# A float32r decoder trunk on one core: 448 unused bytes placed in front of the activation tiles

## The chip, the cores and the metric

The kernel runs on one core of a Trainium2 chip, in one launch. The metric is the device time of one execution in microseconds (us), as the median of several runs. One further execution was recorded by the hardware profiler; all engine times below come from that one. TensorE multiplies matrices, VectorE and ScalarE do elementwise work, GpSimd sets up a small table, and SyncE's queue issues the transfers from the chip's main memory. All of them read their operands from the on-chip memory, which has 128 partitions; a tile takes the same bytes in each partition, so its place is given as a byte within a partition.

## The reference

What is computed is a trunk of four residual layers on 256 tokens of 1024 channels, in float32. Each layer has a token mixer and then a gated convolutional channel mixer (FFN), each with a norm before and after:

```
h = x
for i in range(4):
    a = rms_norm(h, mix_norm_pre[i])
    m = (dilated_attention, short_conv, conformer_conv)[i % 3](a)
    h = h + rms_norm(m, mix_norm_post[i])
    u = causal_dwconv(rms_norm(h, ffn_norm_pre[i]) @ w_in, w_conv)   # width 3
    g, v = split(u)                                                 # 2816 channels each
    h = h + rms_norm((silu(g) * v) @ w_out, ffn_norm_post[i])
```

Layers 0 and 3 mix tokens by attention in three groups of 16 heads (windows 128, 512 and 2048, dilations 1, 4 and 16), whose outputs are weighted by their log-sum-exp. Layer 1 uses a gated convolution of width 3, layer 2 a gated convolution of width 31 with a layer norm. Nearly all of the arithmetic is in the products with the weight matrices.

## The kernel before, in words

Channels lie on the 128 partitions and the 256 tokens along them. A product of the layer's input with a weight matrix is therefore a sum over 8 tiles of 128 input channels (22 in the second FFN product): for each, TensorE loads 128 x 128 weights, and then streams the 128 x 256 inputs past them into a bank of the accumulator memory. The operand that is loaded is called the weights (`lhsT`), the other the stream (`rhs`). For accuracy each float32 operand is split into two float32r parts, `hi` and `lo`, and each product is made of three: hi x hi, hi x lo and lo x hi.

**Weights.** `Stream` (line 145) brings them in, in the order of their use: SyncE's queue loads blocks of 1 MB into one of three `raw` tiles; ScalarE copies a piece of 128 x 1024 into a `whi` tile (line 192), VectorE writes the difference into a `wlo` tile (line 198). The pool `wp` has 11 tiles of each, of 4096 bytes in a partition.

**Activations.** The pool `ap` holds the tiles with the tags `act` (32 buffers of 2048 bytes: 128 x 2 x 256), `tmp` (9 buffers of 1024 bytes) and `tiny` (16 small ones). The function `act` (line 258) takes one, `two` gives the hi and the lo part of an input, each 1024 bytes long, as the two halves of one `act` tile. So the inputs of all large products, the residual's squares, the attention's queries, keys, values and probabilities, and the taps' inputs are `act` tiles.

**Where the tiles lie.** In the order of their opening the pools are `cp` (constants, from byte 16,512), `rawp`, `wp` (from 62,496) and `ap` (from 152,608 to 227,848). Each tile of `raw`, `wp`, `act` and `tmp` has a multiple of 512 bytes, and the pools of these begin 32 past a multiple of 512. So every `whi`, `wlo`, `act` and `tmp` tile begins at byte 32 of 512; so do both halves of an `act` tile, and each slice of 128 columns (512 bytes) of a weight tile. The constants with the identity begin at byte 448 of 512.

**The products.** In `mm3` (lines 279 to 281), in `ramp` (432, 437 and 439: several column tiles at once, while the inputs are being made) and in `Slabs.mm` (521: the second product, summed row slab by row slab) weights of `whi` or `wlo` are loaded and an `act` tile is streamed. In the attention's `value` (877 to 879) it is the other way round: 128 tokens of an `act` tile are loaded, and 256 columns of `whi` or `wlo` are streamed. The other products are smaller: sums of squares (305), token scales spread over channels (323), products of no use that keep TensorE busy at a layer's end (330), taps of the wide convolution as diagonal matrices (714), the mean (723), scores (896), transposes (914) and the weighing of values (925). These work in plain float32, apart from the scores of the first group; a plain float32 product, unlike a transpose, is recorded as two matmuls, a float32r product as one.

**The order of the work** is written out by hand: the whole kernel is issued under `manual_schedule`, each engine does its instructions in the order of the program, and semaphores make it wait for operands and free buffers.

Of the kernel before, what the change touches and what calls it, by code (L numbers as in the profile page):

```python
# [10 lines left out]
F32 = mybir.dt.float32  # L11
# [5 lines left out]
P = 128  # L17
D = 1024
T = 256
# [48 lines left out]
def plan():  # L68
    """The weights in the order of their use, layer by layer: (name, layer, row tile, row tiles, column, columns)."""
    nt = 3 * NH * DH  # L70
    for l in range(DEPTH):
        kind, j = l % 3, l // 3
        if kind == 0:
            for quad in range(NQ):
                for what, g in order(quad):
                    if what == "v":
                        for k0 in (0, 4):
                            yield "attn_w_qkv", j, k0, 4, 2 * nt + (g * NH + 4 * quad) * DH, 2 * P
                    else:
                        c = (g * NH + 4 * quad + 2 * (what == "b")) * DH  # L80
                        yield "attn_w_qkv", j, 0, KD, c, P
                        yield "attn_w_qkv", j, 0, KD, nt + c, P
            for d in range(KD):
                yield "attn_w_o", j, 0, KD, d * P, P
        elif kind == 1:
            for step in sc_steps():
                if step[0] == "col":
                    for c in (D, 2 * D, 0):
                        yield "sc_w_in", j, 0, KD, c + step[1] * P, P
                elif step[0] == "slab":  # L90
                    yield "sc_w_out", j, step[1], 1, 0, D
                elif step[1] % 2 == 0:
                    yield "sc_w_out", j, SC_HEAD, KD - SC_HEAD, step[1] * P, 2 * P
        else:
            for k in range(KD):
                yield "cc_w_pw1", j, 0, KD, k * P, P
                yield "cc_w_pw1", j, 0, KD, D + k * P, P
            for d in range(KD):
                yield "cc_w_pw2", j, 0, KD, d * P, P
        for step in ffn_steps():  # L100
            if step[0] == "col":
                for c in (0, F):
                    yield "ffn_w_in", l, 0, KD, c + step[1] * P, P
            elif step[0] == "slab":
                yield "ffn_w_out", l, step[1], 1, 0, D
            else:
                yield "ffn_w_out", l, FF_HEAD, KF - FF_HEAD, step[1] * P, P


def order(quad):  # L110
    """The blocks of four heads: queries and keys of a pair (a or b), or values of all four, and their group. The
    last values come while the last pair is turned."""
    blocks = "a0 a1 v0 a2 v1 b0 b1 b2 v2" if quad == NQ - 1 else "a0 a1 v0 a2 v1 b0 v2 b1 b2"
    return [(b[0], int(b[1])) for b in blocks.split()]
# [6 lines left out]
def steps(n, head, held, start):  # L121
    """Columns of the first product, and row slabs of the second as their inputs come; the last rows by columns."""
    s = 0
    for i in range(n):
        yield "col", i
        for _ in range(3):
            if i >= start and s <= i - 3 and s < head - held:
                yield "slab", s
                s += 1
    while s < head:  # L130
        yield "slab", s
        s += 1
    for d in range(KD):
        yield "tail", d
# [10 lines left out]
class Stream:  # L145
    """Weights in the order of their use: loaded, then split into two float32r parts."""

# [13 lines left out]
    def add(self, n, room):  # L161
        """A piece of n tiles, in the block that it falls into."""
        if not self.pieces or self.pieces[-1][0] < 0:
            start = 0
        else:
            b, c, m = self.pieces[-1]
            start = b * room + c // P + m
        b, c = divmod(start, room)
        assert c + n <= room
        self.pieces.append((b, c * P, n))  # L170

    def load(self, upto, between=None):
        """Whole blocks; or half a block, something else, and the other half."""
        while self.loaded < min(upto, len(self.blocks)):
# [34 lines left out]
    def pump(self, most=2, margin=1):  # L209
        """Copies one piece ahead of the differences, as far as there is room."""  # L210
        for _ in range(most):
            if self.copied < min(len(self.pieces), self.used - self.held + self.slots - margin):
                self.first()
            if self.prepped < self.copied - 1:
                self.second()
# [13 lines left out]
def trunk_kernel(ctx: ExitStack, tc: tile.TileContext, xT, pos, params, consts, masks, w8, out):  # L229
# [4 lines left out]
    ap = ctx.enter_context(tc.tile_pool(name="ap", bufs=1))  # L234
    ps = ctx.enter_context(tc.tile_pool(name="ps", bufs=1, space=bass.MemoryType.PSUM))

    st = Stream(nc, rawp, wp, SLOTS, 3, [w8[i] for i in range(w8.shape[0])])
    for _, _, _, nk, _, cols in plan():
        st.add(nk * cols // P, 2 * KD)

# [1 line left out]
    par = cp.tile([P, NPAR], F32, name="par")  # L242
# [54 lines left out]

# [1 line left out]
    def rstd_of(accs):  # L299
        """accs [128 channels, T]: sums of squares over channel tiles, eps * D / P with one of them. Returns rstd  # L300
        [128 tokens, 2]."""
        ms = psum("S")
# [16 lines left out]
    def spread(r):  # L319
        """rstd [128 tokens, 2] to all channels: [128, T] in PSUM."""  # L320
        rb = psum("S")[:, :T]
# [10 lines left out]
    def spread_later(r):  # L332
        """The place for the token scale on chip, and what fills it."""
        rb = act()[:, 0, :]
# [5 lines left out]
    def boundary(mg, rb, gain, permuted=False):  # L340
        """The sum into the residual; then the next input: residual * gain in two parts, and the sum of squares.
        The token scale of the next norm follows later."""
        xs = [None] * KD
# [80 lines left out]
    def ramp(xs, os, hook=None):  # L424
        """Column tiles at once, so that the first inputs are used while the next are made. Two that follow each
        other in a bank share its first start."""
        ws = [st.take() for _ in os]
# [20 lines left out]
    def start_norm(xs, acc, os):  # L448
        """The first four column tiles and, beside them, the token scale of their input."""
        r = []  # L450
# [18 lines left out]
    class Out:  # L469
        """The output product's tiles, scaled by the gain of their norm, and the sum of their squares."""  # L470

# [29 lines left out]
        def end(self):  # L501
            """The tiles and their token scale. Meanwhile products of no use keep TensorE's clock up."""
            r = rstd_of(self.acc)
# [5 lines left out]
    class Slabs:  # L509
        """A product accumulated row slab by row slab in four banks, two column tiles to a bank."""  # L510

# [20 lines left out]
        def tail(self, d, xs):  # L532
            """The last rows; where they are few, a piece has the columns of two tiles."""
            e = KD // len(xs)
# [7 lines left out]

# [1 line left out]
    def taps3(srcs, names, ks, between=None):  # L544
# [9 lines left out]

# [1 line left out]
    def ffn(l, mg, rb):  # L556
# [5 lines left out]
        def gate(last=False):  # L562
            """The gate's product with the values, and its parts, a step after their taps."""
            ts = pend.pop(0)
# [46 lines left out]

# [1 line left out]
    def short_conv(l, mg, rb):  # L613
# [43 lines left out]

# [1 line left out]
    def conformer(l, mg, rb):  # L659
# [34 lines left out]
        def taps(q, some):  # L694
            """Taps on VectorE, with the weights' parts between."""
            for i, j in enumerate(some):
# [7 lines left out]
        def products(q, some):  # L704
            """Taps on TensorE, by diagonal matrices."""
            if os[q] is None:
# [82 lines left out]

# [1 line left out]
    SWAP = [(i + 8) % 16 if i < 16 else i for i in range(32)]  # L791

    def attention(l, mg, rb):
# [91 lines left out]
        def scores(pair, c):  # L885
            """Both heads of a pair: their products use different rows of TensorE, and different banks."""
            os = [psum("B") for _ in range(2)]
# [146 lines left out]

# [1 line left out]
    def rotary():  # L1036
        """The tables, with tokens on partitions: on GpSimd the angles and their remainder in three steps; then the
        sines and cosines in the columns that are turned, and the tables on channels."""
        nf = ROT // 2
# [80 lines left out]

# [1 line left out]
def _consts():  # L1122
# [78 lines left out]
```

## Time and profile before

| what | value |
|---|---|
| median of 3 runs | 1616.28 us (1616.08 to 1616.72) |
| the profiled execution: its span, from the first to the last instruction | 1615.5 us |
| the profiled execution: time outside the span | not recorded; the median is 0.8 us above the span |
| TensorE clock granted, mean over the span | 0.995 |
| weights split by VectorE (line 198) | 480 x 1220 ns = 580 us in parallel to TensorE |
| weights copied by ScalarE (line 192) | 480 x 1046 ns = 490 us in parallel to TensorE |
| transfers | 256.94 MB, mean 159 GB/s |

In the profile PE is TensorE's products, PEld its weight loads, which overlap the products, DVE is VectorE, ACT is ScalarE and POOL is GpSimd. A group's row gives the line, the engine, the operation, the tiles written and read with their shapes, the count (x...), then the busy time in us, the mean of one in ns, and the engine's idle time before them with what ended it. A row of the chain or of the timeline gives the start in us, the length in us, and what ran, with the number of instructions merged into it. The rows of stretches give the stretch, its length, and then for each engine the busy us and in parentheses the number of instructions that started; the granted clock, the share of the DMA engines and GB/s follow. Products are pipelined: one starts long before the one ahead of it has ended, so the mean time of one is longer than the distance from start to start.

### The profile page before, as it was taken

The page shows a single profiled execution, that of the slowest core. Times are in us where ns is not written, and L with a number is a line of the kernel's source. Part 1 is how long each engine was busy: PE and PEld are TensorE (multiplying, and loading weights), DVE is VectorE, ACT ScalarE, POOL GpSimd, SP SyncE. Part 2 cuts the span into 40 slices and gives each one's busy share as a digit, 9 for nine tenths or more (in the row PEclk, how much of TensorE's full clock was granted, in tenths as well). Part 3 has the DMA queues.
Part 4 walks back from the last instruction along what each step waited for, and adds up shares of the span by engine and source line. Part 5 has one row for each costly group of instructions (what it writes and reads, how often), then busy time and mean ns, then how long its engine had stood idle before and what let it go on. Part 6 is the DMA issues. An engine that isn't in the chain of part 4 may idle for free.

```text
span 1615.5 us, 31426 instructions
## 1 busy us (share of the span) xinstructions
PE 1589.8 (98%) x13146; PEld 1554.8 (96%) x13146; DVE 1243.3 (77%) x2177; ACT 924.9 (57%) x1623; POOL 18.5 (1%) x51
## 2 busy tenths in 40 slices
PE   6999999999999999999999999999999999999998
PEld 6999999999999999999999999999999999999998
DVE  4987767697876779889599588785877778588783
ACT  6454644575564566556476666565645445566562
POOL 4000000000000000000000000000000000000000
PEclk9999999999999999999999999999999999999999
DMA  5553442265552644655243136553543434236540
GB/s 213 214 213 121 170 144 105 90 235 199 183 185 95 216 157 160 232 183 191 97 150 112 53 127 230 192 183 132 186 180 133 155 131 157 105 131 227 191 157 27
DMA packets 36718, 256.94 MB, mean 159 GB/s; under 512 B 4320, under 2 KB 4448, under 8 KB 5984
## 3 DMA queue, kind: packets, MB, share of 16 engines
q1 hardware_dynamic: 36288, 254.93, 44.0%
q8 instruction: 103, 1.69, 0.4%
q14 instruction: 39, 0.32, 0.1%
q10 hardware_dynamic: 288, 0.01, 0.0%
HBM read 253.87 MB, written 1.05 MB: 158 GB/s over the span
## 4 chain that ended last, share of the span: by engine, by line
PE 95%; DVE 2%; POOL 1%; ACT 1%; DMA 1%; issue 0%; DVEq 0%; POOLq 0%
PE psA L521 17%; PE psB L281 10%; PE psB L280 10%; PE psB L279 10%; PE psA L279 8%; PE psA L280 7%; PE psA L281 7%; PE psA L877 3%; PE psA L879 3%; PE psA L878 3%; PE psB L714 2%; PE psB L896 2%; PE psB L925 2%; PE psA L437 2%; PE psA L432 2%; PE psB L914 2%
## 5 line engine op out<-in xcount | busy, mean ns | idle before, releaser
L198 DVE TENSOR_TENSOR wlo<-raw,whi 128x1024 fp32r<-128x1024 f32 x480 | 579.9, 1220 | 41.8 <-ACT whi L192 40.6
L192 ACT CAST whi<-raw 128x1024 fp32r<-128x1024 f32 x480 | 490.0, 1046 | 22.2 <-DMA raw<-in_w_dram 16.6
L281 PE MATMUL psB<-act,wlo 128*128 128x256 f32 x1392 | 394.2, 283 | 0.0
L280 PE MATMUL psB<-act,whi 128*128 128x256 f32 x1392 | 394.2, 283 | 0.0
L279 PE MATMUL psB<-act,whi 128*128 128x256 f32 x1392 | 394.2, 283 | 0.0
L279 PE MATMUL psA<-act,whi 128*128 128x256 f32 x1040 | 303.6, 292 | 8.0 <-ACT whi L192 7.1
L281 PE MATMUL psA<-act,wlo 128*128 128x256 f32 x1040 | 295.2, 284 | 0.5 <-DVE wlo L198 0.5
L280 PE MATMUL psA<-act,whi 128*128 128x256 f32 x1040 | 295.3, 284 | 0.1
L521 PE MATMUL psA<-act,whi 128*128 128x256 f32 x1536 | 278.0, 283 | 0.0
L279 PEld LDWEIGHTS psB<-act,whi 128*128 128x128 f32 x1392 | 267.4, 192 | 0.0
L281 PEld LDWEIGHTS psB<-act,wlo 128*128 128x128 f32 x1392 | 267.4, 192 | 0.0
L280 PEld LDWEIGHTS psB<-act,whi 128*128 128x128 f32 x1392 | 267.4, 192 | 0.0
L521 PEld LDWEIGHTS psA<-act,whi 128*128 128x128 f32 x1536 | 239.7, 192 | 0.0
L521 PE MATMUL psA<-act,wlo 128*128 128x256 f32 x768 | 217.5, 283 | 0.0
L279 PEld LDWEIGHTS psA<-act,whi 128*128 128x128 f32 x1040 | 200.0, 192 | 12.8 <-ACT whi L192 7.1
L281 PEld LDWEIGHTS psA<-act,wlo 128*128 128x128 f32 x1040 | 200.1, 192 | 0.8 <-DVE wlo L198 0.8
L280 PEld LDWEIGHTS psA<-act,whi 128*128 128x128 f32 x1040 | 200.2, 192 | 0.6 <-DVE act L284 0.5
L290 ACT ACTIVATE tmp<-act,par 128x256 f32<-128x256 f32 x176 | 80.1, 502 | 176.6 <-DVE act L284 176.6
L287 DVE SCALAR_TENSOR_TENSOR tmp<-act,par,tmp 128x255 f32<-128x255 f32 (+1 forms) x352 | 146.6, 478 | 19.7 <-ACT tmp L290 19.7
L521 PEld LDWEIGHTS psA<-act,wlo 128*128 128x128 f32 x768 | 147.5, 192 | 0.0
L284 DVE TENSOR_TENSOR act<-psB,act 128x512 f32<-128x512 f32 (+2 forms) x94 | 58.4, 624 | 101.5 <-PE psB L281 60.1
L877 PE MATMUL psA<-whi,act 128*128 128x256 f32 x384 | 112.4, 293 | 0.0
(124 smaller groups left out, 2129.7 us busy)
## 6 DMA issues: line engine op xcount, KB each, us to landing
raw<-in_w_dram SPq DMA_DIRECT2D x239, 1024.0 KB, 4.8
h<-in_xT_dram SPq DMA_DIRECT2D x4, 256.0 KB, 5.1
raw<-in_w_dram SPq DMA_DIRECT2D x2, 512.0 KB, 5.5
out_dram<-h SPq DMA_DIRECT2D x4, 256.0 KB, 2.1
msk<-in_masks_dram SPq DMA_DIRECT2D x1, 512.0 KB, 9.4
par<-in_params_dram SPq DMA_DIRECT2D x1, 484.0 KB, 10.1
cst<-in_consts_dram SPq DMA_DIRECT2D x1, 132.0 KB, 5.9
par<-in_params_dram ACTq DMA_DIRECT2D x1, 4.0 KB, 2.9
```

Source lines behind the costliest of these rows:

```text
L192: self.nc.scalar.copy(out=hi, in_=raw)
L198: self.nc.vector.tensor_tensor(out=lo, in0=raw, in1=hi.bitcast(F32), op=ALU.subtract)
L279: nc.tensor.matmul(o, lhsT=whi, rhs=x[0], start=first, stop=False)
L280: nc.tensor.matmul(o, lhsT=whi, rhs=x[1], start=False, stop=False)
L281: nc.tensor.matmul(o, lhsT=wlo, rhs=x[0], start=False, stop=last)
L284: nc.vector.tensor_tensor(out=out, in0=a, in1=b, op=op)
L287: nc.vector.scalar_tensor_tensor(out=out, in0=a, scalar=s, in1=b, op0=op0, op1=op1)
L290: nc.scalar.activation(out=out, in_=a, func=AF.Identity, scale=s, bias=b)
L521: nc.tensor.matmul(o, lhsT=a, rhs=b, start=first and i == 0, stop=last and i == 2, skip_group_check=True)
L877: nc.tensor.matmul(oc, lhsT=xh, rhs=whi[:, k % 4, :], start=k == 0, stop=False)
L878: nc.tensor.matmul(oc, lhsT=xh, rhs=wlo[:, k % 4, :], start=False, stop=False)
L879: nc.tensor.matmul(oc, lhsT=xl, rhs=whi[:, k % 4, :], start=False, stop=k == KD - 1)
```

## The change

One tile of 112 float32 numbers (448 bytes in a partition) is taken from the activation pool `ap`, before any other. Nothing writes or reads it.

```
     ap = ctx.enter_context(tc.tile_pool(name="ap", bufs=1))
     ps = ctx.enter_context(tc.tile_pool(name="ps", bufs=1, space=bass.MemoryType.PSUM))
+    ap.tile([P, 112], F32, tag="gap", name="gap")
 
     st = Stream(nc, rawp, wp, SLOTS, 3, [w8[i] for i in range(w8.shape[0])])
```

All `act`, `tmp` and `tiny` tiles then lie 448 bytes higher: `act` and `tmp` tiles begin at byte 480 of 512, the weight tiles stay at byte 32, the constants at 448. The rest of the diff takes out comments and docstrings; the added line moves the numbers of all lines below it by one. No instruction is added, removed or moved on any engine.

More of the change, by code (lines that the diff above doesn't have):

```diff
@@ L235, in trunk_kernel @@
     ps = ctx.enter_context(tc.tile_pool(name="ps", bufs=1, space=bass.MemoryType.PSUM))
+    ap.tile([P, 112], F32, tag="gap", name="gap")
     st = Stream(nc, rawp, wp, SLOTS, 3, [w8[i] for i in range(w8.shape[0])])
```

## The prediction

> **What bounds the kernel now.** I read the page's first lines first: how long, which engine, at what clock.
>
> ```profile
> span 1615.5 us, 31426 instructions
> PE 1589.8 (98%) x13146; PEld 1554.8 (96%) x13146; DVE 1243.3 (77%) x2177; ACT 924.9 (57%) x1623; POOL 18.5 (1%) x51
> PEclk9999999999999999999999999999999999999999
> ```
>
> TensorE is never without work and its clock is granted in full. VectorE, next, has 372 us to spare. The chain that ended last says the same:
>
> ```profile
> PE 95%; DVE 2%; POOL 1%; ACT 1%; DMA 1%; issue 0%; DVEq 0%; POOLq 0%
> ```
>
> So the end is set by how closely one product follows another. The groups give the number of products; the mean time of one (283 ns) is no pace, since products overlap.
>
> ```profile
> L279 PE MATMUL psB<-act,whi 128*128 128x256 f32 x1392 | 394.2, 283 | 0.0
> L279 PE MATMUL psA<-act,whi 128*128 128x256 f32 x1040 | 303.6, 292 | 8.0 <-ACT whi L192 7.1
> L521 PE MATMUL psA<-act,whi 128*128 128x256 f32 x1536 | 278.0, 283 | 0.0
> L521 PE MATMUL psA<-act,wlo 128*128 128x256 f32 x768 | 217.5, 283 | 0.0
> L877 PE MATMUL psA<-whi,act 128*128 128x256 f32 x384 | 112.4, 293 | 0.0
> L437 PE MATMUL psA<-act,whi 128*128 128x256 f32 x256 | 65.3, 289 | 0.4 <-ACT act L290 0.2
> ```
>
> Lines 279, 280 and 281 issue 2432 each, 521 issues 2304, the three lines of `ramp` (432, 437, 439) 256 each: 7296 + 2304 + 768 = 10,368 products in float32r stream 256 columns of an activation tile (1024 bytes in a partition) past 128 columns of weights. Lines 877 to 879 issue 3 x 384 = 1152 more the other way round: the activations are loaded as weights and the weight tile streams. Together 11,520.
>
> The pace stands in the chain in order of time, where unbroken runs are merged:
>
> ```profile
> 461.17 34.57 PE psA L521 x288
> 818.30 11.23 PE psB L714 x52
> 887.95 3.47 PE psS L723 x16
> ```
>
> 34.57 / 288 is 120.0 ns from one float32r product to the next, and 11,520 x 120.0 is 1382 us of the 1615.5. The plain float32 products of lines 714 and 723 (256 columns in two records of 216 and 217 ns) and the rest fill the other 233 us. The span lies 0.8 us below the median of the three runs, 1616.28; I take these 0.8 us as fixed.
>
> **What 120.0 ns is made of.** The edit can act only through this number, so I look for what sets it. Two rows show the parts by themselves: four transposes, each streaming 128 float32 columns, and twenty weight loads of 128 columns whose products stream a single column.
>
> ```profile
> 78.53 0.60 PE L914 MATMUL psB<-cst,act 128*128 128x128 f32 x4
> ...
> 894.04 2.31 PEld L305 LDWEIGHTS psS<-cst,act 128*128 128x128 f32 x20 [0.45 <-ACT act L751]
> ...
> L914 PE MATMUL psB<-cst,act 128*128 128x128 f32 x256 | 38.4, 273 | 0.0
> L305 PEld LDWEIGHTS psS<-cst,act 128*128 128x128 f32 x20 | 2.3, 192 | 0.4 <-ACT act L751 0.4
> ```
>
> The transposes start (0.60 - 0.273) / 3 = 109 ns apart. The loads start (2.31 - 0.192) / 19 = 111.5 ns apart, with hardly a stream beside them. Float32r needs 120.0: 8.5 ns more than loads alone, 11 more than the closest stream.
>
> Two explanations fit. One: the stream is read in pieces. 108 ns (half of line 714's 216) for 1024 bytes are eight pieces of 128 bytes at 13.5 ns; from byte 32 the 1024 bytes touch nine pieces, and 9 x 13.5 is 121 ns. Plain float32 spends two of these times on the same bytes, so a ninth piece would not show. Two: stream and load are both under way at once, and one makes the other wait some 8.5 ns in each product, because both begin at byte 32 of 512. In the trace of before every float32r stream and load begins there, so no row parts the two.
>
> [...]
>
> **The change, part by part.**
>
> *The gap tile.* It is never written or read: no instruction, no DMA. In the built program every engine has the same instructions in the same order. Cost 0. The pool ends 448 bytes higher, at byte 228,296, and still fits.
>
> *10,368 streams from byte 480 instead of 32, weights still at 32.* By the pieces, 1024 bytes from 480 touch nine of 128 bytes again (480 is 96 past a multiple of 128), as they do from 32. Of 64 bytes they touch 17 both times, of 256 five, of 512 three. Whatever the size of a piece, both starts lie off its edge or both on it: 10,368 x 0 = 0. From both sides: the best that a row allows is the loads' pace alone, 111.5 ns, so 10,368 x 8.5 = 88 us less (at the transposes' 109 it would be 114 less); the worst I bound by one more piece, 13.5 ns each, 140 us more. I take 0, since what the trace shows of TensorE's paces depends on how much is read and not on where. The rows are those of line 714: its fifteen taps stream from fifteen starts, bytes 100 to 156 of 512 (36 to 92 after), past weights at byte 32, and the run of 52 keeps 216.0 ns; line 723 streams from byte 32 past weights at 448, and has 217.
>
> *1152 value products.* Their stream stays at byte 32, their load moves to 480. By the pieces 0; by the second explanation they, too, change, with the opposite sign of distance. At most 1152 x 8.5 = 10 us either way.
>
> *Other products on moved tiles* (transposes, scores, weighing, taps, the mean) are plain float32, and by line 714's row they do not mind: 0. 192 scores products are float32r; 8.5 ns in each would be under 2 us.
>
> *VectorE and ScalarE* read and write the moved tiles too. VectorE's taps start at a new byte each, and the time follows the number of elements alone:
>
> ```profile
> L287 DVE SCALAR_TENSOR_TENSOR act<-act,par,act 128x240 f32<-128x240 f32 x8 | 3.3, 452 | 0.0
> L287 DVE SCALAR_TENSOR_TENSOR act<-act,par,act 128x235 f32<-128x235 f32 x8 | 3.3, 448 | 0.0
> L287 DVE SCALAR_TENSOR_TENSOR act<-act,par,act 128x230 f32<-128x230 f32 x8 | 3.3, 445 | 0.0
> ```
>
> Under 1 ns an element, no step among them: 0. A slower VectorE would be covered by its 372 us of slack in most stages. DMAs touch none of the moved tiles.
>
> Sum: 1615.5 + 0, plus 0.8 around it: 1616.3 us.
>
> **Rivals.** *Faster: the two reads collide, and the shift parts them.* A load takes 111.5 / 128 = 0.87 ns for each 4 bytes, a stream at most 120 / 256 = 0.47. Started together at byte 32, the stream would leave the load's place at once and come round to it, 512 bytes on, near the product's end: two meetings. Begun 64 bytes behind the load's place, it overtakes once, early. For it: 120 ns has no part in it that a row shows alone. Against it: VectorE and ScalarE use the same memory, and their traffic leaves no mark on the pace:
>
> ```profile
> 461.00:495.00 34.00, 34.00 (x286) 34.00 (x285) 20.09 (x28) 20.12 (x33) 0.00 (x0) 1.00 0.52 187
> 1030.00:1064.00 34.00, 34.00 (x286) 34.00 (x285) 29.16 (x48) 19.35 (x32) 0.00 (x0) 1.00 0.51 184
> ```
>
> 286 products (second column) in each 34 us, though VectorE (fourth column) was busy 20.09 and 29.16 us. A memory that makes its readers queue by address should make those queue too. Price: at 111.5 ns 88 us less, 1528; one meeting of two removed, 44 less, 1572; at 109 ns 114 less, 1502. VectorE would stand at 1243 / 1528 = 81%, so it stays covered except where it is full already:
>
> ```profile
> 620.00:660.00 40.00, 40.00 (x336) 40.00 (x335) 40.00 (x64) 29.54 (x45) 0.00 (x0) 1.00 0.70 255
> ```
>
> Here it worked all 40 us, and a faster TensorE would wait for it.
>
> [...]
>
> *Slower: the first piece is too short.* From byte 480 only 32 bytes, 8 columns, come before a boundary of 512 (and of 128); from 32 there are 480 (or 96). If the stream needs the next piece sooner than it can come, TensorE stands still at each product's start. It decides from the point where this standstill exceeds what already lies idle within the 120 ns: the stream itself uses 108 of them, so 12 ns. Price: half a piece, 6.75 x 10,368 = 70 us, 1686; a whole one, 140 us, 1756. For it: nothing in the trace covers such a start. Against: line 714's starts 116 to 124 leave 12 to 4 bytes before a multiple of 128, without a mark, though at half the rate.
>
> *The change does not do what it says.* If the pool put the gap last, nothing would move. The built program has the first activation tile at byte 153,056, which is 480 past a multiple of 512, and the weight tiles still at 32. Excluded.
>
> **The numbers.** No change 0.52: the pieces fit 120 ns to 1%, and no row reacts to a start address. Faster 0.28, slower 0.20, since every float32r row has the same start and the evidence is from other kinds of product. The likeliest gives 1616.3; its own range is 1613 to 1620 (0.2%, 3.2 us, is about what a measurement of this kernel can tell from no change). With the faster rival down to 1502 the range 1502 to 1620 holds 0.80 and leaves out the slower.
>
> **What would show it.** Right: L521's run of 288 again takes 34.6 us (120.0 ns) and the value products 120. The first rival: that run under 33.9 us, the gain in all lines 279 to 281, 432 to 439 and 521, VectorE above 77%, and value products differing from the others. The second: that run over 35 us with lines 877 to 879 unchanged. A change in the plain float32 runs (216 ns), or in VectorE's taps, would make my reasoning wrong from the start.

## The result and the profile after

The changed kernel took 1580.70 us in the median of 4 runs (1576.42 to 1584.66), the kernel before 1616.18 in the median of 4 (1615.73 to 1616.72). The ratio is 0.9777 (95% interval 0.9764 to 0.9791): 35.5 us faster, where no change was forecast. The time lies outside the 1613 to 1620 of the likeliest case, and inside the wide range only because that was drawn down to 1502 for the first rival. The changed kernel also scatters eight times as much as the one before, 8.2 us against 1.0; the experiments come back to this.

The page of the changed kernel (its own time 1583.57 us, the span below):

```profile
span 1581.7 us, 31426 instructions
PE 1555.7 (98%) x13146; PEld 1520.5 (96%) x13146; DVE 1243.0 (79%) x2177; ACT 925.2 (58%) x1623; POOL 17.9 (1%) x51
PEclk9999999999999999999999999999999999999999
PE 93%; DVE 3%; ACT 1%; POOL 1%; issue 1%; DMA 1%; DVEq 0%; ACTq 0%; POOLq 0%
```

The counts are the same, VectorE and ScalarE are as busy as before, the clock is still full, and the end is still TensorE's. Its busy time alone went down, from 1589.8 to 1555.7 us: 34.1, all that the span lost (33.8). So the products follow one another more closely. The chain in order of time, changed kernel; all four long runs of `Slabs.mm` (now line 522), a run of plain float32 taps (715) and the mean (724):

```profile
451.09 33.93 PE psA L522 x288
739.31 33.93 PE psA L522 x288
801.30 11.23 PE psB L715 x52
870.55 3.47 PE psS L724 x16
1063.45 33.94 PE psA L522 x288
1536.55 33.93 PE psA L522 x288
```

33.93 / 288 is 117.8 ns where 120.0 stood. The plain float32 runs keep 11.23 and 3.47 us to the last digit. The mean distance from start to start in the trace, products that wait left out, fell in each group of float32r products: `mm3` went from 119.85 to 116.59 ns, `Slabs.mm` from 120.01 to 117.78, `ramp` from 119.90 to 115.52, the value products from 119.61 to 116.73. Times their 7296, 2304, 768 and 1152 these make 23.8 + 5.1 + 3.4 + 3.3 = 35.6 us. That accounts for the 33.8 that this execution's span lost and is slightly too much, in part because the sum gives the gain also to products that begin after a wait. In `mm3`, `ramp` and the value products the distances are not spread around the mean: nearly all are 113 or 114 ns, or 117 to 119. In `Slabs.mm` all are 117 to 119.

### The profile page after: what moved, and what is told of

It reads as the page before. It is cut to its first block, busy times and chain, and to the rows that moved or that the text cites. A ratio compares the mean times of both kernels' runs of the same rounds, so it can differ in the third digit from the quotient of the medians.

```text
span 1581.7 us, 31426 instructions
## 1 busy us (share of the span) xinstructions
PE 1555.7 (98%) x13146; PEld 1520.5 (96%) x13146; DVE 1243.0 (79%) x2177; ACT 925.2 (58%) x1623; POOL 17.9 (1%) x51
## 4 chain that ended last, share of the span: by engine, by line
PE 93%; DVE 3%; ACT 1%; POOL 1%; issue 1%; DMA 1%; DVEq 0%; ACTq 0%; POOLq 0%
PE psA L522 17%; PE psB L282 10%; PE psB L280 10%; PE psB L281 10%; PE psA L280 7%; PE psA L281 7%; PE psA L282 7%; PE psA L878 3%; PE psA L880 3%; PE psA L879 3%; PE psB L715 2%; PE psB L926 2%; PE psB L897 2%; PE psA L438 2%; PE psB L915 2%; PE psA L433 2%
## 5 line engine op out<-in xcount | busy, mean ns | idle before, releaser
L192 ACT CAST whi<-raw 128x1024 fp32r<-128x1024 f32 x480 | 490.9, 1048 | 23.8 <-DMA raw<-in_w_dram 18.7
L280 PE MATMUL psA<-act,whi 128*128 128x256 f32 x1040 | 299.2, 288 | 8.0 <-ACT whi L192 7.1
L282 PE MATMUL psA<-act,wlo 128*128 128x256 f32 x1040 | 290.7, 280 | 0.5 <-DVE wlo L198 0.5
L281 PE MATMUL psA<-act,whi 128*128 128x256 f32 x1040 | 290.8, 280 | 0.2
L522 PE MATMUL psA<-act,whi 128*128 128x256 f32 x1536 | 272.9, 281 | 0.0
L281 PEld LDWEIGHTS psB<-act,whi 128*128 128x128 f32 x1392 | 265.0, 190 | 0.0
L282 PEld LDWEIGHTS psB<-act,wlo 128*128 128x128 f32 x1392 | 263.1, 189 | 0.0
L280 PEld LDWEIGHTS psB<-act,whi 128*128 128x128 f32 x1392 | 261.3, 188 | 0.0
L522 PEld LDWEIGHTS psA<-act,whi 128*128 128x128 f32 x1536 | 236.2, 189 | 0.0
L522 PE MATMUL psA<-act,wlo 128*128 128x256 f32 x768 | 215.8, 281 | 0.0
L280 PEld LDWEIGHTS psA<-act,whi 128*128 128x128 f32 x1040 | 196.9, 189 | 12.8 <-ACT whi L192 7.1
L282 PEld LDWEIGHTS psA<-act,wlo 128*128 128x128 f32 x1040 | 197.1, 190 | 0.8 <-DVE wlo L198 0.8
L281 PEld LDWEIGHTS psA<-act,whi 128*128 128x128 f32 x1040 | 197.2, 190 | 0.6 <-DVE act L285 0.5
L522 PEld LDWEIGHTS psA<-act,wlo 128*128 128x128 f32 x768 | 145.2, 189 | 0.0
```

The lines of the kernel that those rows point to most:

```text
L192: self.nc.scalar.copy(out=hi, in_=raw)
L280: nc.tensor.matmul(o, lhsT=whi, rhs=x[0], start=first, stop=False)
L281: nc.tensor.matmul(o, lhsT=whi, rhs=x[1], start=False, stop=False)
L282: nc.tensor.matmul(o, lhsT=wlo, rhs=x[0], start=False, stop=last)
L522: nc.tensor.matmul(o, lhsT=a, rhs=b, start=first and i == 0, stop=last and i == 2, skip_group_check=True)
```

## The theories

*Distance.* The pace is set by how far the stream's start lies from that of the weights that are being loaded beside it: the two reads get in each other's way. Before, the distance was 0; now it is 448 (or -64, the same modulo 512) for the inputs past their weights, and 64 for the value products, where the parts are swapped.

*Start.* The stream's own start sets it, and byte 480 is better than 32.

*Pieces*, the theory of the prediction: the number of 128-byte pieces that the stream touches. It gave no change for byte 480, and there it has failed; an input that begins at a multiple of 128 bytes, with eight pieces, can still test it.

## First experiments: what sets the pace

The first experiment puts weights and inputs both at byte 480. The unused bytes stand in front of the weight tiles, and the pool behind them moves along:

```
-    ap.tile([P, 112], F32, tag="gap", name="gap")
+    wp.tile([P, 112], F32, tag="wgap", name="wgap", bufs=1)
```

> The 448 unused bytes stand in front of the weight tiles, so weights and inputs both begin at byte 480 and their distance is 0 again. If the distance between the two starts sets the pace (reads that meet), the run of 288 products of Slabs.mm is back at 34.6 us (120.0 ns) and the time at 1616. If the input's own start sets it, that run stays at 33.9 us (117.8 ns) and the time at 1576 to 1585, as in the changed kernel.

Measured: 1616.75 us, ratio 1.0001 (0.9992 to 1.0010). Its chain:

```profile
461.13 34.57 PE psA L522 x288
```

Back to 120.0 ns with inputs at 480: the start theory is out.

The second puts the weights at 96 and the inputs at 32:

```
+    wp.tile([P, 16], F32, tag="wgap", name="wgap", bufs=1)
     ap.tile([P, 112], F32, tag="gap", name="gap")
```

> 64 unused bytes in front of the weight tiles and 448 more in front of the activations: weights begin at byte 96, inputs at byte 32 as before, distance -64 as in the changed kernel. Distance theory: 1576 to 1585, 117.8 ns in the run of 288 and 113 to 118 ns elsewhere. Start theory: 120.0 ns and 1616, since the input begins where it began before.

Measured: 1557.07 us (1555.55 to 1558.44), ratio 0.9633 (0.9618 to 0.9647). With the distance of the changed kernel, and the inputs where they were before, the kernel is fast again. But it is faster than expected, and `Slabs.mm` has another pace:

```profile
446.82 32.66 PE psA L523 x288
```

32.66 / 288 is 113.4 ns, in all four long runs, against 117.8 in the changed kernel. The distance is not all, then.

The next two put the inputs at 0 (`[P, 120]` for the gap) and at 288 (`[P, 64]`):

> 480 unused bytes: inputs begin at byte 0 of 512, weights at 32, distance -32. The pieces theory of the prediction: eight pieces in place of nine, 108 to 109 ns a product, about 1500. Distance theory: the two reads start half as far apart as in the changed kernel, so a pace between 117.8 and 120.0 ns and 1580 to 1616, and nothing special about an aligned start.

> 256 unused bytes: inputs begin at byte 288, weights at 32, distance 256, half of 512. Distance theory with a period of 512: the reads meet neither at the start nor at the end, one meeting in the middle, pace at or below the changed kernel's 113 to 118 ns, 1540 to 1585. With a period of 256 the distance is 0 again: 120.0 ns and 1616. Pieces theory: 120.0 ns and 1616.

Measured: 1597.74 us for the inputs at 0, ratio 0.9884 (0.9869 to 0.9898), and 1616.49 for those at 288, ratio 1.0000 (0.9990 to 1.0010). The chain of the first, then that of the second:

```profile
456.79 34.10 PE psA L522 x288
```

```profile
461.25 34.57 PE psA L522 x288
```

An aligned start gives 118.4 ns, not 108: pieces of 128 bytes are out. And at a distance of 256 the pace is 120.0 again, to the digit: if distance counts, it counts modulo 256, not 512.

## The pace measured by itself

The next kernel leaves out the whole trunk. It runs 48 float32r products of 256 columns in a row, waits for ScalarE to fetch the sum, and does so six times for each pair of starts (`line` is not used):

```
+    def run(name, line, w0, x0, cols=P, n=T, count=48, again=6):
+        for _ in range(again):
+            o = ps.tile([P, 512], F32, tag="o", name=name)
+            for i in range(count):
+                w = ws[:, w0 // 4 + (i % 8) * P:][:, :cols]
+                x = xs[:, x0 // 4 + (i % 5) * T:][:, :n]
+                nc.tensor.matmul(o[:cols, :n], lhsT=w, rhs=x, start=i == 0, stop=i == count - 1)
+            nc.scalar.copy(out=ev[:cols, :n], in_=o[:cols, :n])
```

> This kernel computes nothing of the trunk: it measures the pace of float32r products by itself. 48 products of 256 columns with 128 weights in an unbroken row, then a wait, six times for each pair of starts; weights start at byte 32 (at 96 in four more), inputs 0, 16, 32 ... 480 bytes after them, modulo 512. The name says the distance and the weights' start. Pieces theory: 108 ns where the input's start is a multiple of 128, 120 ns everywhere else. Distance theory: 120.0 ns at 0 and 256, since the two kernels with these distances had 120.0, 113 or 118 ns at 64 and 448, 118 on average at 480, the same at 64 and 448 with the weights at 96, and either a second lowest pace or another 120.0 at 128 and 384, which says whether the period is 256 or 128. Two rows with only 32 columns of weights to load: if it is the load that collides with the stream, 107 to 109 ns at every distance; if the stream alone is slow, 120 at distance 0. Two with 64 and 128 streamed columns: the pace of loads, 107 to 112 ns.

These are rows of its timeline, of TensorE alone; the name says distance and weights' start, and each row is one run of 48. Only the lengths (second column) are to be compared with each other; they hold the slower first products and the end of the last:

```profile
30.77 6.01 PE L245 MATMUL d0w32s<-xs,ws 128*128 128x256 f32 x48 [0.52 <-ACT ev L246]
...
108.15 5.92 PE L245 MATMUL d64w32s<-xs,ws 128*128 128x256 f32 x48 [0.52 <-ACT ev L246]
...
263.50 5.71 PE L245 MATMUL d192w32s<-xs,ws 128*128 128x256 f32 x48 [0.52 <-ACT ev L246]
...
339.95 6.01 PE L245 MATMUL d256w32s<-xs,ws 128*128 128x256 f32 x48 [0.52 <-ACT ev L246]
...
417.33 5.92 PE L245 MATMUL d320w32s<-xs,ws 128*128 128x256 f32 x48 [0.52 <-ACT ev L246]
...
572.68 5.71 PE L245 MATMUL d448w32s<-xs,ws 128*128 128x256 f32 x48 [0.52 <-ACT ev L246]
...
919.91 5.71 PE L245 MATMUL d448w96s<-xs,ws 128*128 128x256 f32 x48 [0.52 <-ACT ev L246]
```

0 and 256, 64 and 320, 192 and 448 are the same, and so are the other five pairs of the scan: the period is 256. Whether the weights start at 32 or at 96 does not count. Of the rows with 32 columns to load neither expected outcome came: at distance 0 they had 117.8 and 113.3 ns in turn, where 128 columns have 120.0. So the load does cost the stream something, but a shorter one does not bring 107 to 109 ns. A second scan has steps of 16 and other starts of the weights:

> Pace by itself again, nothing of the trunk is computed: distances 0 to 240 in steps of 16 with the weights at bytes 0, 16 and 48, six distances with them at 32, and four rows (c1) whose load has one column, so that the stream is nearly alone. Distance theory: the paces of the first scan at each distance, whatever the weights' start: 120.0 at 0, 113.3 at 112 and 192. Pieces of 64 bytes (1024 bytes from a multiple of 64 are 16 pieces of 6.67 ns, else 17): with the weights at 0 the distance 192 gives 106.7 ns, and with one column the stream has 106.7 ns from byte 0 and 64 and 113.3 from bytes 16 and 32. If 113.3 is instead what the start of any load costs the stream, the one-column rows keep 113.3 at every start.

The steady pace in ns (from the 13th start of a run to the last), weights at byte 0 or 32, both scans; where runs of one distance differ, both values stand:

| distance modulo 256 | 0 | 16 | 32 | 48 | 64 | 80 | 96 | 112 |
|---|---|---|---|---|---|---|---|---|
| pace | 120.0 | 116.6 / 118.7 | 116.6 | 118.3 | 117.8 | 118.3 / 120.0 | 120.1 | 113.3 |

| distance modulo 256 | 128 | 144 | 160 | 176 | 192 | 208 | 224 | 240 |
|---|---|---|---|---|---|---|---|---|
| pace | 118.7 / 120.0 | 118.7 | 117.3 / 118.7 | 119.2 | 113.3 / 117.8 | 119.2 | 118.3 | 117.1 |

With the weights at 16 or 48 the paces are others (112 has 118.3 or 120.0 there), while 192 has 113.3 in all six runs: between weights at 0 or 32 and weights at 16 or 48 the start does count. The distance of the changed kernel, 448, is 192 modulo 256, one of the two best; its pace is one of two, as the runs of the second scan show one by one. Two rows of its timeline with the weights at 0, then two whose load has a single column (c1, with the inputs' start):

```profile
256.15 5.93 PE L245 MATMUL d192w0s<-xs,ws 128*128 128x256 f32 x48 [0.52 <-ACT ev L246]
262.59 5.73 PE L245 MATMUL d192w0s<-xs,ws 128*128 128x256 f32 x48 [0.52 <-ACT ev L246]
...
1081.61 5.60 PE L245 MATMUL c1x0s<-xs,ws 128*1 128x256 f32 x48 [0.51 <-ACT ev L246]
...
1106.17 5.60 PE L245 MATMUL c1x32s<-xs,ws 128*1 128x256 f32 x48 [0.51 <-ACT ev L246]
```

The first run at this distance settled on 117.8 ns, the next on 113.3: the same instructions on the same addresses, after a wait of the same length. A row of products falls into one of two rhythms within its first products after a wait, and keeps it. It does not look like mere chance: in the first scan the six runs at 128 and the six at 384 have the same paces in the same order (118.7 three times, 119.9, 120.0, 118.7).

With a single column to load, the stream has 113.3 ns from byte 0 and from byte 32 (of the 12 runs from four starts three had 116.6 to 117.8). The weights lie at byte 32 in these rows, so c1x32 has distance 0, where 128 columns of load make 120.0: at this distance the time is lost through the load. No distance went below 113.3, so this is as far as the remedy goes, and pieces of 64 bytes, which would have given 106.7 from byte 0, are out as well. Of the 12 runs with 64 and 128 streamed columns 11 had half the clock (0.50 granted); the first began at the full clock, at 112 ns, which is the loads' pace of the prediction.

## The two rhythms in the trunk

The next kernel has the inputs at 224 (`[P, 48]` for the gap), a distance of 192:

> 192 unused bytes in place of 448: inputs begin at byte 224, distance 192, which is 448 modulo 256. Distance theory with a period of 256: nothing but the chance of which of the two paces (113.3 or 117.8 ns) a stretch falls into tells it from the changed kernel, 1555 to 1585. With a period of 512 it would be an untried distance, with the pace open. Start theory: 1616, unless byte 224 happens to be another good start.

Measured: 1573.86 us (1566.42 to 1577.45), ratio 0.9734 (0.9699 to 0.9768). Its chain shows both rhythms in one execution:

```profile
445.96 32.66 PE psA L522 x288
732.89 33.93 PE psA L522 x288
...
1057.10 33.93 PE psA L522 x288
1525.02 32.66 PE psA L522 x288
```

Then the changed kernel was run once more, and the distance -64 a third time (`[P, 32]` in front of the weights, `[P, 112]` in front of the activations):

> The changed kernel itself once more, beside the other three on one chip. Two-paces theory: each of the four long unbroken stretches of the channel mixer (some 1480 products) falls into 113.3 or 117.8 ns after the wait ahead of it and stays there; that is 4.45 ns x 1480 = 6.6 us a stretch, so the times lie on steps of 6.6 us between 1557 (all four fast, as in the second experiment) and 1584 (all four slow, as in the profile of the changed kernel). One-pace theory: the scatter is of another kind, with a profile of 117.8 ns throughout in all four.

> 128 unused bytes in front of the weights and 448 in front of the activations: weights at 160, inputs at 96, distance -64 for a third time, both starts new. Distance and two-paces theory: 1555 to 1585 on the same steps of 6.6 us. If the absolute start decided between the second experiment (1557) and the changed kernel (1580), nothing ties this one to either end.

Measured: 1584.13 us (1583.90 to 1584.74), ratio 0.9801 (0.9786 to 0.9816), for the changed kernel, which this time hardly scattered, and 1569.73 for the other, in runs of 1563.41, 1566.49, 1572.96 and 1583.43, ratio 0.9723 (0.9673 to 0.9773). In the profiles the trunk has five unbroken stretches of over 400 products, four of 1478 in the channel mixers and one of 662; each has one rhythm throughout (mean distance in ns):

| kernel (profiled execution) | 1478 | 662 | 1478 | 1478 | 1478 | us |
|---|---|---|---|---|---|---|
| weights 96, inputs 32 | 113.3 | 113.3 | 113.3 | 113.3 | 113.3 | 1557.15 |
| weights 160, inputs 96 | 113.3 | 117.8 | 117.8 | 113.3 | 113.3 | 1566.49 |
| inputs 224 | 113.3 | 117.8 | 117.8 | 117.8 | 113.3 | 1570.76 |
| changed kernel | 117.8 | 117.8 | 117.8 | 117.8 | 117.8 | 1583.57 |
| changed kernel, again | 117.8 | 117.8 | 117.8 | 117.8 | 117.8 | 1584.33 |

From the first row, 6.6 us for each slow long stretch and 2.9 for the short one give 1566.7, 1573.3 and 1586.5 for the next three, against 1566.5, 1570.8 and 1583.6: the number of stretches in the slow rhythm explains most of the difference between these kernels. The scatter within the changed kernel fits it too, since its two faster runs, 1576.42 and 1577.84, lie about one long stretch below 1583.57; but those two executions have no profile, so this is not shown. That number does not look like mere chance in a given kernel (all five slow in both of the changed kernel's profiles, all five fast in the one profile at 96 and 32); what decides it was not found.

At distance 112 all nine runs of the scans (weights at 0 or 32) settled on 113.3. In the trunk this needs starts 16 bytes off the pools' steps of 32, hence larger tiles, and room for them (an excerpt; the change of `SLOTS` alone, without unused bytes, is the control):

```
-SLOTS = 11
+SLOTS = 10
...
+    ap.tile([P, 24], F32, tag="gap", name="gap")
...
+        if tag == "act":
+            t = ap.tile([P, 2 * T + 64], dt, tag=tag, name=f"{tag}{counter[0]}", bufs=bufs)
+            return t[:, 4:2 * T + 4].rearrange("p (s t) -> p s t", s=2)
```

> The kernel before with 10 in place of 11 tiles for the weights' parts, with no unused bytes: a control for the next one, which needs the room. TensorE's pace is 120.0 ns; the time is 1616 if the eleventh tile hides nothing, some us more if it does.

> 10 weight tiles, activation tiles of 2304 bytes in place of 2048 with the data from byte 16 of them, and 96 unused bytes in front: weights at 32, all inputs at 144 or 400, distance 112 modulo 256, the one at which every run of the scans came to 113.3 ns. Distance theory: 113.3 ns in all stretches, 10,368 x 6.67 = 69 us less than the control, and the value products (distance 144) at 118.7: 1546 if the control has 1616, with little scatter. If the trunk's order of work decides the pace and not the distance, a mix of 113.3 and 117.8 as in the changed kernel, 1555 to 1585.

Measured: the control took 1621.76 us, ratio 1.0032 (1.0020 to 1.0043); distance 112 has 1564.51 (1564.29 to 1565.00), ratio 0.9679 (0.9663 to 0.9696). Chain of distance 112:

```profile
448.28 32.66 PE psA L525 x288
728.34 32.66 PE psA L525 x288
...
1048.68 32.66 PE psA L525 x288
1518.85 32.66 PE psA L525 x288
```

Every long stretch has the fast rhythm, and the scatter is small (0.7 us). The gain is 57 us over the control, not 69. `mm3` has 113.94 ns on average, as the first nine distances after a wait are 116.5 on average; the value products (119.86, at distance 144) gained nothing. By their paces the groups make 43.0 + 15.4 + 4.2 - 0.3 = 62 us. Of the other 5 us, 3.7 are time in which TensorE had no product: the span less its busy time is 27.6 us in the control and 31.3 here. Weights at 96 and inputs at 32 remain the fastest version that was run, at 1557.07, though nothing found here says why that layout kept the fast rhythm.

## Why the prediction was wrong

*The sum.* Reading the bound was right: 1382 us of products that follow each other set the time, and the gain came from their pace. The step that failed is the value taken for the 10,368 streams: "I take 0, since what the trace shows of TensorE's paces depends on how much is read and not on where." The paces show that it does depend on where: by the groups above, the term came to 32.3 us less in place of 0 (35.6 with the value products), a good third of the 88 that the prediction gave as its best end. What sets the pace first of all is the distance between the two starts, modulo 256.

*Its evidence.* Line 714's fifteen starts at one pace were read rightly, and its runs of 52 take 11.23 us in every kernel here with 11 weight tiles. (Its weights are `tmp` tiles of the same pool, so these kernels move both its operands together and its distances stay; line 723's distance does change, and its products still start 216 ns apart.) But such a record takes 216 ns for the same 1024 bytes. A ninth piece was allowed to hide in it; a collision should have been allowed the same, and the rows then say nothing on float32r. The float32r products in question had a single distance, 0, so the trace was silent, and silence was counted as an argument for no change.

*The pieces.* 9 x 13.5 fitting 120 ns to 1% was a coincidence: an aligned start had 118.4 ns in the trunk, and a stream with almost no load has 113.3 from aligned and other starts alike.

*The first rival.* Its mechanism, load and stream in each other's way by their distance, is the one that the runs bear out as far as they go: distance alone brings back 120.0 (both at 480) or takes it away (weights moved in place of inputs), and with a single column to load distance 0 costs nothing. That the two reads meet at an address, once or twice in a product, is not shown. Wrong were its period, 256 and not 512, and its size: 2.2 or 6.7 ns a product, not 8.5, since no distance comes below 113.3. Its figure for one of two meetings removed, 1572, was near by luck: the two rhythms are no such half. The argument against it, that other engines' traffic leaves the pace alone, still holds after, and never spoke of TensorE's own two reads. This is the changed kernel in a stretch with VectorE busy 39.27 of 40 us:

```profile
610.00:650.00 40.00, 40.00 (x342) 40.00 (x342) 39.27 (x61) 29.14 (x43) 0.00 (x0) 1.00 0.71 251
```

It has 342 products in 40 us where the prediction's row of such a stretch has 336, although VectorE has hardly a gap. (The counts in these rows, here and in the prediction, also hold the two or three products under way at the edges.) VectorE did not become the bound there, as was feared; with weights at 96 and inputs at 32 it worked all 40 us from 600 to 640, beside 356 products.

The Trainium skill ("TensorE: Matmul & The Clock Gate", Part 2, "Step-by-step: what each phase is for") says that the streaming operand and the weight load have independent read ports, and that loading the next weights takes no read bandwidth from the running product. What the ports do no run shows. The consequence does not hold here: at distance 0 products with 128 columns to load are 120.0 ns apart and products with a single one 113.3, so loading slows the running products, by up to 6.7 ns.

*The second rival* is out: no start in the scans made the steady pace slower than 120.1.

*The signs named beforehand.* The run of 288 under 33.9 us was to mean the first rival; it came to 33.93, a hair above, because all stretches of that execution were in the slow rhythm. VectorE's taps were to stay and did not, which the prediction named as a fault in its reasoning from the start; the last section has their rows.

*What stays open*: which of the two reads is held up and by what; why the lowest pace is 113.3 ns and not 108, half of what a plain float32 record takes; why the period is 256 bytes; why a stretch takes the one or the other rhythm.

## What to carry to other kernels

Where TensorE's products with different weights follow each other without a gap, look up the starts of both operands modulo 256. Here, with float32r, 128 columns of weights and 256 streamed columns, the layout that falls out by itself (all tiles at the same start) had the slowest pace but for 0.1 ns, and a few hundred unused bytes that made the distance 192 modulo 256 cut the time by 2 to 4%. A row that does not react is evidence only if it would have shown the effect; a product at half the rate does not. When a pace is constant to the digit in one layout and comes in two values in another, compare profiles stretch by stretch before taking an average for the effect.

## What else the runs showed

VectorE's long taps took longer as well. These are the three rows of the prediction, in the changed kernel:

```profile
L288 DVE SCALAR_TENSOR_TENSOR act<-act,par,act 128x240 f32<-128x240 f32 x8 | 3.4, 480 | 0.0
L288 DVE SCALAR_TENSOR_TENSOR act<-act,par,act 128x235 f32<-128x235 f32 x8 | 3.4, 469 | 0.0
L288 DVE SCALAR_TENSOR_TENSOR act<-act,par,act 128x230 f32<-128x230 f32 x8 | 3.3, 462 | 0.0
```

480, 469 and 462 ns stand where 452, 448 and 445 stood; with inputs at 0 it was 450, 446 and 442, at 224 511, 496 and 484. The taps' own start is not all of it: with weights at 96 and inputs back at 32 they took 468, 461 and 456. In the changed kernel the busy time of all 132 of these taps grew by 0.4 us (50.8 to 51.2), which the time does not feel; the cause was not tried.
